# A decoder layer on one core: plain chunks moved inside a column pair, the tail of an up block spread, the residual kept in DRAM, a sixth raw tile

## The chip, the core and the metric

The kernel runs on one core of one Trainium2 chip. The core has a matrix engine (TensorE, PE in the profile; its weight loads are PEld), VectorE (DVE), ScalarE (ACT), GpSimd (POOL) and a queue processor (SyncE, SP), each with an instruction stream of its own. They wait for each other by semaphores. SP issues most of the DMA transfers, GpSimd the accumulating ones. The metric is the device time of one execution in microseconds; the figure compared is the median of the runs.

## The reference

One layer on 256 tokens of width 2048, in float32:

```
hn = rmsnorm(h);  q, k, v, g_ret, xr, yr, g_a, g_b = split(hn @ w_in)
ret_out = silu(g_ret) * head_groupnorm(chunkwise_retention(rotary(q), rotary(k), v))   # 8 heads
rnn_out = gelu(yr) * rg_lru(causal_dwconv(xr))
h = h + (sigmoid(g_a) * (ret_out @ w_proj_ret) + sigmoid(g_b) * (rnn_out @ w_proj_rnn)) @ w_mix_out
h = h + cross_attention(rmsnorm(h), rmsnorm(mem))          # 4 heads, 256 memory tokens
gate, val = split(causal_dwconv(rmsnorm(h) @ w_up, 3 taps))   # 2 x 5632 wide
h = h + (silu(gate) * val) @ w_down
return rmsnorm(h)
```

## The kernel before

**Products.** Every operand is split into two float32r parts, hi and lo, and a product is hi*hi + hi*lo + lo*hi. The weights come from DRAM as one long stream of pieces of 1 MB: four 128-row blocks by 512 columns (a chunk). A chunk is loaded into a `raw` tile (L263), cast to `hi` on ScalarE (L284), and VectorE writes `lo = raw - hi` (L285). `prefetch` does this two chunks ahead of their use. There are five raw tiles and three each of `hi` and `lo`.

**Column pairs.** Two 512-column blocks that share rows form a pair, listed in `PAIR_UNITS`. The first half of the contraction (rows 0 to 7) is done with seven block products on sums of operands (q1 to q7, a form of Strassen's scheme), the second half (rows 8 to 15) with four plain chunks (p). A q chunk takes 12 matmuls (one of them handles 512 columns), a p chunk 24. Three raw tiles, A, B and C, are held through a pair: q5 adds a piece to A by an accumulating DMA on GpSimd's queue (L265), then VectorE does A += B (L292); q6 uses A; q7 adds a piece to B by the same kind of DMA; VectorE does A += C (L290), and q4 uses A. The order in time is q1, p, q3, p, q5, q2, q6, p, q7, q4, p. Three PSUM accumulators serve a pair: xz, yu and rw; each holds [128, 2, 512]. There are three such tiles in all, and each chunk of a single column block (`gemm_n`) or of a transposed product (`gemm_t`) takes from the same three.

**Which p does what.** In the kernel before, p comes as (column 1, rows 8 to 11), (column 1, rows 12 to 15), (column 0, rows 8 to 11), (column 0, rows 12 to 15). Column 1 adds to rw, column 0 to yu. `pair_add` adds the accumulators to the residual rows `hrow` (L427), `pair_out` writes them to new tiles (L454 to L472).

**Order of work.** `later(n, fn)` puts a piece of side work n chunks ahead. The tile framework then orders each engine's instructions by priorities when the program is built; each engine runs its own list in that order. Tiles of the pool `bp` (25 of 4 KB per partition) hold operands, residual rows and the like; `tp` holds ten short-lived ones.

**Retention.** The eight heads come in two groups. In a group, q, k and v are computed, then a pair for the gates (`pair_out` at `O_G`). v of the first group is a `gemm_n`; `split_rows` reads its accumulator in two halves (L563 on ScalarE, L564 on VectorE). `retain` does the scores of a head (L518 on TensorE, L768, L769 on VectorE into `pret`), then the values; at the fourth head `normalise` takes the rsqrt (L608 on VectorE, the power L610 on GpSimd, L796) and scales the rows; `finish_head` transposes them (L530).

**Feed-forward.** `FF_PARTS` has groups of 4, 4 and 3 up blocks. An up block b is two `gemm_t` products, gate and value (`conv_up`): the accumulators are joined and scaled (L540, L541, L672), and a causal convolution of three taps follows (L1187, L1189). Then tanh (L1257), two products (L1258, L1259) and the split into a pair of `hid` tiles (L551, L552). In the first two groups `sums` makes the operands of the q chunks from the first four. A group of four is followed by two pairs of `ffn_w_down`, whose last quarter of the contraction is the two `hid` tiles of the fourth up block. The last group is followed by four plain `gemm_n`. All four `hrow` tiles stay in SBUF from cross-attention on.

Of the kernel before, what the change touches and what calls it, by code (L numbers as in the profile page):

```python
# [27 lines left out]
BW = 512  # L28
KC = 4
KH = 2  # L30
RAW_BUFS = 5
PART_BUFS = 3
AHEAD = 2
WARM = 8
# [60 lines left out]
def residual_plan(w):  # L95
# [5 lines left out]

PAIR_UNITS = [
    ("q1", "A", ("new", 0, 0)),
    ("p", None, (1, 8)),
    ("q3", "B", ("new", 1, 1)),
    ("p", None, (1, 12)),
    ("q5", "A", ("add", 0, 1)),
    ("q2", "C", ("new", 1, 0)),
    ("q6", "A", ("sum",)),
    ("p", None, (0, 8)),  # L110
    ("q7", "B", ("add", 0, 1)),
    ("q4", "A", ("sum",)),
    ("p", None, (0, 12)),
]

def entry_units(e):

    w, row, nk, cols = e[0], e[1], e[2], e[3:5]
    if len(cols) == 1:
        return [("p", None, "new", (w, tuple(row + (k + i) * P for i in range(KC)), cols[0])) for k in range(0, nk, KC)]  # L120
    out = []
    for kind, slot, a in PAIR_UNITS:
        if kind == "p":
# [29 lines left out]
def hybrid_layer(  # L153
# [17 lines left out]

    cp = ctx.enter_context(tc.tile_pool(name="cp", bufs=1))
    wp = ctx.enter_context(tc.tile_pool(name="wp", bufs=2))
    bp = ctx.enter_context(tc.tile_pool(name="bp", bufs=25))
    tp = ctx.enter_context(tc.tile_pool(name="tp", bufs=10))
    sp_ = ctx.enter_context(tc.tile_pool(name="sp", bufs=2))
    pm = ctx.enter_context(tc.tile_pool(name="pm", bufs=3, space=bass.MemoryType.PSUM))
# [205 lines left out]
    def pair_products(w, row, st, ss, c0, c1, out):  # L383

        xz, yu, rw = acc(), acc(), acc()
        x, z, y, u, r, w_ = (t[:, i, :] for t in (xz, yu, rw) for i in range(2))
        where = {
            "q1": (x, "a", 0, 0), "q2": (y, "a", 1, 0), "q3": (r, "s", 3, 0), "q4": (u, "a", 1, 1),
            "q5": (z, "s", 0, 0), "q6": (x, "s", 1, 0), "q7": (x, "s", 2, 0),
        }  # L390
        begun, plain = set(), 0

        def run(os_, opss, parts):
            for o, ops in zip(os_, opss):
                upper_n(o[0], ops, parts, o[1] not in begun)
                begun.add(o[1])
            for o, ops in zip(os_, opss):
                lower_n(o[0], ops, parts, True)

        names = {"q1": "x", "q2": "y", "q3": "r", "q4": "u", "q5": "z", "q6": "x", "q7": "x"}  # L400
        e = (w, row, NT, c0, c1)
        for kind, parts in units(*e):
            if kind == "p":
                k0 = 8 + 4 * (plain % 2)
                run(
                    (((r, "r"), (w_, "w")), ((y, "y"), (u, "u")))[plain // 2],
                    [
                        [halves(st[(k0 + k) // 2], k % 2, slice(tt * P, (tt + 1) * P)) for k in range(KC)]
                        for tt in range(2)
                    ],  # L410
                    parts,
                )
                plain += 1
            else:
                o, t, j, tt = where[kind]
                if t == "a":
                    ops = [halves(st[k], j, slice(tt * P, (tt + 1) * P)) for k in range(KC)]
                else:
                    ops = [(ss[k][:, 0, j * P : (j + 1) * P], ss[k][:, 1, j * P : (j + 1) * P]) for k in range(KC)]
                run(((o, names[kind]),), (ops,), parts)  # L420
            with tc.high_priority(URGENT):
                out(f"p{plain}" if kind == "p" else kind, x, z, yu, rw)

    def pair_add(w, row, st, ss, c0, c1, h0, h1):

        def add(o, i, op=ALU.add):
            dve.tensor_tensor(out=o, in0=o, in1=i, op=op)  # L427

        def out(kind, x, z, yu, rw):
            if kind == "q1":  # L430
                add(h0[:, 0, :], x)
            elif kind == "q5":
                later(3, lambda: add(h1, rw))
                later(4, lambda: add(h1, z[:, None, :].to_broadcast([P, 2, BW])))
            elif kind == "q6":
                add(h1[:, 0, :], x, ALU.subtract)
            elif kind == "q7":
                add(h0[:, 1, :], x)
                add(h1[:, 1, :], x, ALU.subtract)
            elif kind == "p4":  # L440
                add(h0, yu)

        pair_products(w, row, st, ss, c0, c1, out)

    def pair_out(w, st, ss, c0, r=None):
# [30 lines left out]
        def out(kind, x, z, yu, rw):  # L476
            if kind == "q1":
                copy(o0[:, 0, :], x, 0)
            elif kind == "q5":
                for tt in range(2):  # L480
                    copy(o1[:, tt, :], z, tt)
                later(3, lambda: add(o1, rw))
            elif kind == "q6":
                less(o1[:, 0, :], x, 0)
            elif kind == "q7":
                copy(o0[:, 1, :], x, 1)
                less(o1[:, 1, :], x, 1)
            elif kind == "p4":
                add(o0, yu)

        pair_products(w, 0, st, ss, c0, c0 + BW, out)
# [264 lines left out]
    def retain(g, qr, kr, vs, dec, gates):  # L756
# [4 lines left out]
        def scores(hh):  # L761
# [2 lines left out]
            product(sc[:, 0:S], halves(k, hh % 2, slice(0, P)), halves(q, hh % 2), True, True)  # L764
            late = slice(P, S)
            product(sc[:, S : S + P], halves(k, hh % 2, late), halves(q, hh % 2, late), True, True)
            pr_ = tp.tile([P, 384], F32, tag="pret", bufs=2, name=nm("pret"))
            dve.tensor_tensor(out=pr_[:, 0:S], in0=sc[:, 0:S], in1=dec[:, hh, :], op=ALU.mult)  # L768
            dve.tensor_tensor(out=pr_[:, S:384], in0=sc[:, S:384], in1=dec[:, hh, 0:P], op=ALU.mult)  # L769
            phi, plo = (tp.tile([P, 384], F32R, tag="tmp", name=nm("ps")) for _ in range(2))  # L770
# [4 lines left out]
        def values(hh, phi, plo):  # L775
# [12 lines left out]
                dve.bn_aggr(out=stats[:, 2 * hh + tt, :], in_=bn[:, tt, :])  # L788
            raws.append(rc)
            if hh == 3:  # L790
                later(2, normalise)

        def normalise():
            rstd = rsqrt_small(stats[:, :, 1], 8, 1.0, GN_EPS).rearrange("p (h t) -> p h t", t=2)
            for tt in range(2):
                dve.tensor_scalar_mul(rstd[:, :, tt], rstd[:, :, tt], rs0[:, tt : tt + 1])  # L796
# [381 lines left out]
    later(1, lambda: spread_tokens(rs2))  # L1178


    def conv_up(c0, b, dst):
        for pr, a in enumerate(gemm_t("ffn_w_up", 0, h2s, NT, c0 + b * BW)):
            z = scaled(a, "uz")
            for j in range(2):
                t = c0 // P + 4 * b + 2 * pr + j
                y = dst[:, 2 * pr + j, :]
                act.activation(y, z[:, j, :], AF.Identity, scale=pf[:, 2, t : t + 1], bias=pf[:, 3, t : t + 1])  # L1187
                for s in range(1, 3):
                    dve.scalar_tensor_tensor(  # L1189
                        out=y[:, s:S], in0=z[:, j, 0 : S - s], scalar=pf[:, 2 - s, t : t + 1], in1=y[:, s:S],  # L1190
                        op0=ALU.mult, op1=ALU.add,
                    )

    def down(b0, hid, b, final):

# [43 lines left out]
    def finish(b):  # L1239

        for tt in range(2):
            y = hrow[b][:, tt, :]
            square(y, ss3[:, tt, b : b + 1])
            dve.tensor_tensor(out=y, in0=y, in1=wfin[b // 2][:, b % 2, :], op=ALU.mult)

    b0 = 0
    for part, nb_ in enumerate(FF_PARTS):
        final = part == len(FF_PARTS) - 1
        hid, hid_sums = [], []
        for b in range(b0, b0 + nb_):  # L1250
            gt, vl = big([P, 4, S], s="fg"), big([P, 4, S], s="fv")
            conv_up(0, b, gt)
            conv_up(FF, b, vl)
            for pr in range(2):
                cs = slice(2 * pr, 2 * pr + 2)
                th, o = tmp("ft"), tmp("fo")
                act.activation(th, gt[:, cs, :], AF.Tanh, scale=0.5)  # L1257
                dve.scalar_tensor_tensor(out=o, in0=th, scalar=1.0, in1=gt[:, cs, :], op0=ALU.add, op1=ALU.mult)  # L1258
                dve.tensor_tensor(out=o, in0=o, in1=vl[:, cs, :], op=ALU.mult)  # L1259
                hid.append(split_pair(o, 0.5))  # L1260
                if nb_ == 4 and len(hid_sums) < KC:
                    hid_sums.append(sums(o, 0.5))
        if final:
            wfin = []
            for i in range(2):
# [48 lines left out]
```

## Time and profile before

| | |
|---|---|
| runs | 2009.12, 2009.64, 2011.54 us; median 2009.64 |
| profiled execution | 2011.54 us, span 2009.8 us |
| instructions | 24882 |
| DMA | 430.97 MB, mean 214 GB/s |
| granted TensorE clock | 0.998 on average |

The page has busy times by engine, the span in 40 slices, DMA queues, the chain that ended last, and groups of instructions. A row of the instructions in order of time reads: start, duration, engine, line, operation, output<-inputs, shape, count; in brackets the idle time of that engine before it and what ended it. Successive matmuls overlap in these rows: a matmul's own duration is about 0.39 us, while in a full stream starts follow each other at shorter distance, so lengths are taken from start to start.

### The profile page before, as it was taken

What the parts mean: (1) busy time and instruction counts of PE and PEld (TensorE: products, weight loads), DVE (VectorE), ACT (ScalarE), POOL (GpSimd) and SP (SyncE); (2) the same over time, 40 slices, a digit from 0 to 9 for tenths busy, and PEclk for the clock granted to TensorE, in tenths of its full rate; (3) what the DMA queues carried; (4) which work ended last, traced back from release to release, by engine and by line L of the source; (5) the groups of instructions that cost most, each with busy time, mean ns of one, the idle gap of its engine ahead of it and who ended that gap; (6) DMA issues with size and microseconds to landing.
All of it is one profiled execution on the core that took longest, in us unless ns stands there. A gap on an engine that the chain in (4) does not pass through costs nothing.

```text
span 2009.8 us, 24882 instructions
## 1 busy us (share of the span) xinstructions
PE 1989.9 (99%) x10072; PEld 1691.7 (84%) x10072; DVE 1585.2 (79%) x1588; ACT 1158.7 (58%) x1167; POOL 43.0 (2%) x52
## 2 busy tenths in 40 slices
PE   9999999999999999999999999999999999999998
PEld 7888888888888888888888888888878888788887
DVE  6798797889985886768888768777787787886765
ACT  6565656767665554566766556555544555544552
POOL 0000000000000000000000000000000000000000
PEclk9999999999999999999999999999999999999999
DMA  9664674655977775877886647655567555584552
GB/s 369 237 226 140 229 245 176 210 202 145 295 245 246 214 246 189 262 249 234 267 246 204 254 130 223 233 187 196 182 197 238 194 189 188 170 264 173 200 198 84
DMA packets 76003, 430.97 MB, mean 214 GB/s; under 512 B 8304, under 2 KB 13040, under 8 KB 28144
## 3 DMA queue, kind: packets, MB, share of 16 engines
q1 hardware_dynamic: 68608, 384.81, 52.2%
q0 software_dynamic: 5760, 41.95, 11.5%
q10 hardware_dynamic: 1520, 2.63, 0.4%
q8 instruction: 79, 1.29, 0.2%
q14 instruction: 36, 0.29, 0.0%
HBM read 418.87 MB, written 10.49 MB: 214 GB/s over the span
## 4 chain that ended last, share of the span: by engine, by line
PE 91%; DVE 5%; DMA 1%; issue 1%; ACT 1%; POOL 0%; SPq 0%; POOLq 0%; ACTq 0%; DVEq 0%
PE acc L349 37%; PE acc L360 17%; PE acc L361 17%; PE acc L367 16%; DVE lo L285 2%; PE sm L518 2%; DMA raw<-in_wall 1%; PE sm L530 1%; ACT hi L284 1%; PE acc L518 1%; PE sm L892 1%; DVE raw L292 0%; DVE fv L1189 0%; DVE tb L718 0%; DMA xt<-in_mem_t 0%
## 5 line engine op out<-in xcount | busy, mean ns | idle before, releaser
L285 DVE TENSOR_TENSOR lo<-raw,hi 128x2048 fp32r<-128x2048 f32 (+1 forms) x420 | 950.7, 2268 | 299.1 <-ACT hi L284 286.0
L284 ACT CAST hi<-raw 128x2048 fp32r<-128x2048 f32 (+1 forms) x418 | 792.8, 1902 | 624.1 <-PE acc L361 292.6
L360 PE MATMUL acc<-hi,s 128*128 128x512 f32 x1336 | 523.3, 392 | 4.3 <-ACT hi L284 3.9
L361 PE MATMUL acc<-hi,s 128*128 128x512 f32 x1336 | 520.7, 390 | 0.2 <-DVE s L575 0.2
L349 PE MATMUL acc<-s,hi 128*128 128x512 f32 x2176 | 518.0, 391 | 2.2 <-DVE hi L282 1.1
L349 PEld LDWEIGHTS acc<-s,hi 128*128 128x128 f32 x2176 | 401.9, 188 | 82.1 <-ACT hi L284 1.8
L367 PE MATMUL acc<-lo,s 128*128 128x512 f32 x1336 | 340.1, 392 | 0.1
L360 PEld LDWEIGHTS acc<-hi,s 128*128 128x128 f32 x1336 | 251.0, 188 | 58.0 <-ACT hi L284 5.2
L367 PEld LDWEIGHTS acc<-lo,s 128*128 128x128 f32 x1336 | 250.1, 188 | 53.6 <-DVE lo L285 0.5
L361 PEld LDWEIGHTS acc<-hi,s 128*128 128x128 f32 x1336 | 251.0, 188 | 52.2 <-DVE s L575 1.0
L349 PEld LDWEIGHTS acc<-s,lo 128*128 128x128 f32 x2176 | 277.0, 191 | 9.9 <-DVE lo L285 1.3
L349 PE MATMUL acc<-s,lo 128*128 128x256 f32 x2176 | 282.9, 283 | 0.5 <-DVE lo L285 0.5
L360 PE MATMUL acc<-hi,ss 128*128 128x512 f32 x320 | 127.2, 397 | 3.6 <-DVE o L470 1.7
L361 PE MATMUL acc<-hi,ss 128*128 128x512 f32 x320 | 125.5, 392 | 0.0
L367 PE MATMUL acc<-lo,ss 128*128 128x512 f32 x320 | 86.0, 390 | 0.0
L540 ACT COPY c<-acc 128x512 f32<-128x512 f32 x68 | 39.2, 578 | 75.2 <-PE acc L349 74.9
L360 PEld LDWEIGHTS acc<-hi,ss 128*128 128x128 f32 x320 | 60.6, 189 | 18.2 <-ACT hi L284 2.5
L361 PEld LDWEIGHTS acc<-hi,ss 128*128 128x128 f32 x320 | 60.6, 189 | 12.2
L367 PEld LDWEIGHTS acc<-lo,ss 128*128 128x128 f32 x320 | 60.0, 188 | 12.7
L265 POOL DMA_DIRECT2D raw<-in_wall x40 | 35.2, 879 | 1574.2 <-DVE lo L285 845.2
L427 DVE TENSOR_TENSOR nat<-nat,acc 128x512 f32<-128x512 f32 (+1 forms) x49 | 44.0, 910 | 6.7 <-PE acc L367 6.7
L290 DVE TENSOR_TENSOR raw<-raw,raw 128x2048 f32<-128x2048 f32 x20 | 45.8, 2288 | 0.4
(233 smaller groups left out, 1242.6 us busy)
## 6 DMA issues: line engine op xcount, KB each, us to landing
raw<-in_wall SPq DMA_DIRECT2D x333, 1024.0 KB, 4.9
raw<-in_wall POOLq DMA_DIRECT2D x40, 1024.0 KB, 8.0
xt<-in_x_t SPq DMA_DIRECT2D x11, 256.0 KB, 7.0
raw<-in_wall SPq DMA_DIRECT2D x5, 512.0 KB, 8.5
nat<-in_x ACTq DMA_DIRECT2D x4, 512.0 KB, 9.8
ret<-hd SPq DMA_DIRECT2D x8, 256.0 KB, 5.1
rnn<-rn SPq DMA_DIRECT2D x8, 256.0 KB, 3.1
kt<-ret SPq DMA_DIRECT2D x8, 256.0 KB, 5.6
```

The lines of the kernel that those rows point to most:

```text
L265: pool.dma_start(out=raw, in_=src, accum_op=ALU.add)
L284: act.copy(hi[:, a:b], raw[:, a:b])
L285: dve.tensor_tensor(out=lo[:, a:b], in0=raw[:, a:b], in1=hi[:, a:b].bitcast(F32), op=ALU.subtract)
L290: dve.tensor_tensor(out=to, in0=to, in1=by, op=ALU.add)
L349: pe.matmul(a, part, sx, start=k == 0 and t == 0, stop=k == nk - 1 and t == 0, skip_group_check=True)
L360: pe.matmul(o, h, hi, start=start and kk == 0, stop=False, skip_group_check=True)
L361: pe.matmul(o, l, hi, start=False, stop=False, skip_group_check=True)
L367: pe.matmul(o, h, lo, start=False, stop=stop and kk == KC - 1, skip_group_check=True)
L427: dve.tensor_tensor(out=o, in0=o, in1=i, op=op)
L518: pe.matmul(o, a, b, start=start and i == 0, stop=stop and i == 2, skip_group_check=True)
L530: pe.transpose(t[:, j, tt * P : (tt + 1) * P], rows[:, tt, k + j * P : k + (j + 1) * P], ident)
L540: act.copy(c, a[:, :, S:BW])
```

## The change

- **Plain chunks.** In `PAIR_UNITS` the four p units get names p0 to p3 and another order: (column 1, rows 8 to 11), (column 0, rows 8 to 11), (column 1, rows 12 to 15), (column 0, rows 12 to 15). The last quarter of the contraction is now used by the third and fourth p. q units and all positions stay.
- **Last up block.** `conv_up` is parted into `up` (product, join, scale) and `conv`; tanh, products and split go into `hidden`. In the fourth up block of a group of four, `conv` of the value half and `hidden` are put behind the second and the fourth chunk of the first `ffn_w_down` pair; else they run at once. In all up blocks both halves are joined and scaled before the first convolution.
- **Residual.** Before the first up block `hrow` is written to DRAM (`fkept`), and read back in the last up block of each group: all four in the last group, else two there and two in the first pair (after its fifth chunk). After each pair of `ffn_w_down` its two blocks are written again. All this goes by SP's queue.
- **Tiles.** `RAW_BUFS` 5 to 6, `bp` 25 to 24; `pret` takes its tile from the common tag `tmp` and no longer from two of its own.
- **Retention.** `normalise` is parted: the rsqrt runs one chunk earlier than before, the rest one chunk later.

```diff
-RAW_BUFS = 5
+RAW_BUFS = 6
...
 PAIR_UNITS = [
     ("q1", "A", ("new", 0, 0)),
-    ("p", None, (1, 8)),
+    ("p0", None, (1, 8)),
     ("q3", "B", ("new", 1, 1)),
-    ("p", None, (1, 12)),
+    ("p1", None, (0, 8)),
     ("q5", "A", ("add", 0, 1)),
     ("q2", "C", ("new", 1, 0)),
     ("q6", "A", ("sum",)),
-    ("p", None, (0, 8)),
+    ("p2", None, (1, 12)),
     ("q7", "B", ("add", 0, 1)),
     ("q4", "A", ("sum",)),
-    ("p", None, (0, 12)),
+    ("p3", None, (0, 12)),
 ]
...
-    bp = ctx.enter_context(tc.tile_pool(name="bp", bufs=25))
+    bp = ctx.enter_context(tc.tile_pool(name="bp", bufs=24))
...
+        rows = {"p0": (8, (r, "r"), (w_, "w")), "p1": (8, (y, "y"), (u, "u"))}
+        rows.update({"p2": (12,) + rows["p0"][1:], "p3": (12,) + rows["p1"][1:]})
...
-            elif kind == "p4":
+            elif kind == "p3":
...
-            pr_ = tp.tile([P, 384], F32, tag="pret", bufs=2, name=nm("pret"))
+            pr_ = tp.tile([P, 384], F32, tag="tmp", name=nm("pret"))
...
-                later(2, normalise)
-
-        def normalise():
+                later(1, rsqrt)
+
+        def rsqrt():
             rstd = rsqrt_small(stats[:, :, 1], 8, 1.0, GN_EPS).rearrange("p (h t) -> p h t", t=2)
+            later(1, lambda: normalise(rstd))
+
+        def normalise(rstd):
...
+    def up(c0, b):
+        return [scaled(a, "uz") for a in gemm_t("ffn_w_up", 0, h2s, NT, c0 + b * BW)]
+
+    def conv(c0, b, pr, z, dst):
+        for j in range(2):
...
+    def put_rows(n, bs):
+        for b in bs:
+            sp.dma_start(out=fkept[n, b], in_=hrow[b])
+
+    def get_rows(n, bs):
+        for b in bs:
+            hrow[b] = big([P, 2, BW], s="nat")
+            sp.dma_start(out=hrow[b], in_=fkept[n, b])
+
+    def hidden(gt, vl, pr, summed):
...
+    put_rows(0, range(4))
...
         for b in range(b0, b0 + nb_):
             gt, vl = big([P, 4, S], s="fg"), big([P, 4, S], s="fv")
-            conv_up(0, b, gt)
-            conv_up(FF, b, vl)
...
+            for pr, z in enumerate(up(0, b)):
+                conv(0, b, pr, z, gt)
+            if b + 1 == b0 + nb_:
+                later(0, lambda part=part, n=2 if paired else 4: get_rows(part % 2, range(n)))
+            for pr, z in enumerate(up(FF, b)):
+                def finish_up(b=b, pr=pr, z=z, gt=gt, vl=vl, paired=paired):
+                    conv(FF, b, pr, z, vl)
+                    hidden(gt, vl, pr, paired)
+
+                if paired and b + 1 == b0 + nb_:
+                    later(1 + 2 * pr, finish_up)
+                else:
+                    finish_up()
...
             for b in (0, 2):
+                if b == 0:
+                    later(4, lambda part=part: get_rows(part % 2, (2, 3)))
                 pair_add("ffn_w_down", b0 * BW, hid, hid_sums, b * BW, (b + 1) * BW, hrow[b], hrow[b + 1])
+                put_rows((part + 1) % 2, (b, b + 1))
```

More of the change, by code (lines that the diff above doesn't have):

```diff
@@ L122, in entry_units @@
     for kind, slot, a in PAIR_UNITS:
-        if kind == "p":
+        if kind[0] == "p":
             out.append((kind, slot, "new", (w, tuple(row + (a[1] + i) * P for i in range(KC)), cols[a[0]])))
@@ L390, in pair_products @@
         }
-        begun, plain = set(), 0
+        rows = {"p0": (8, (r, "r"), (w_, "w")), "p1": (8, (y, "y"), (u, "u"))}
+        rows.update({"p2": (12,) + rows["p0"][1:], "p3": (12,) + rows["p1"][1:]})
+        begun = set()
         def run(os_, opss, parts):
@@ L402, in pair_products @@
         for kind, parts in units(*e):
[L403 to L413, printed above, removed]
+            if kind in rows:
+                k0, *to = rows[kind]
+                ops = [
+                    [halves(st[(k0 + k) // 2], k % 2, slice(tt * P, (tt + 1) * P)) for k in range(KC)]
+                    for tt in range(2)
+                ]
+                run(to, ops, parts)
             else:
@@ L421, in pair_products @@
             with tc.high_priority(URGENT):
-                out(f"p{plain}" if kind == "p" else kind, x, z, yu, rw)
+                out(kind, x, z, yu, rw)
     def pair_add(w, row, st, ss, c0, c1, h0, h1):
@@ L487, in out @@
                 less(o1[:, 1, :], x, 1)
-            elif kind == "p4":
+            elif kind == "p3":
                 add(o0, yu)
@@ L1178, in hybrid_layer @@
     later(1, lambda: spread_tokens(rs2))
[L1181 to L1192, printed above, removed]
+    def up(c0, b):
+        return [scaled(a, "uz") for a in gemm_t("ffn_w_up", 0, h2s, NT, c0 + b * BW)]
+    def conv(c0, b, pr, z, dst):
+        for j in range(2):
+            t = c0 // P + 4 * b + 2 * pr + j
+            y = dst[:, 2 * pr + j, :]
+            act.activation(y, z[:, j, :], AF.Identity, scale=pf[:, 2, t : t + 1], bias=pf[:, 3, t : t + 1])
+            for s in range(1, 3):
+                dve.scalar_tensor_tensor(
+                    out=y[:, s:S], in0=z[:, j, 0 : S - s], scalar=pf[:, 2 - s, t : t + 1], in1=y[:, s:S],
+                    op0=ALU.mult, op1=ALU.add,
+                )
     def down(b0, hid, b, final):
@@ L1244, in finish @@
             dve.tensor_tensor(out=y, in0=y, in1=wfin[b // 2][:, b % 2, :], op=ALU.mult)
+    fkept = dp.tile([2, 4, P, 2, BW], F32, name="fkept")
+    def put_rows(n, bs):
[6 more added lines that the diff above has]
+    def hidden(gt, vl, pr, summed):
+        cs = slice(2 * pr, 2 * pr + 2)
+        th, o = tmp("ft"), tmp("fo")
+        act.activation(th, gt[:, cs, :], AF.Tanh, scale=0.5)
+        dve.scalar_tensor_tensor(out=o, in0=th, scalar=1.0, in1=gt[:, cs, :], op0=ALU.add, op1=ALU.mult)
+        dve.tensor_tensor(out=o, in0=o, in1=vl[:, cs, :], op=ALU.mult)
+        hid.append(split_pair(o, 0.5))
+        if summed and len(hid_sums) < KC:
+            hid_sums.append(sums(o, 0.5))
+    put_rows(0, range(4))
     b0 = 0
@@ L1248, in hybrid_layer @@
         final = part == len(FF_PARTS) - 1
+        paired = nb_ == 4
         hid, hid_sums = [], []
@@ L1251, in hybrid_layer @@
             gt, vl = big([P, 4, S], s="fg"), big([P, 4, S], s="fv")
-            conv_up(0, b, gt)
-            conv_up(FF, b, vl)
[L1254 to L1262, printed above, removed]
+            for pr, z in enumerate(up(0, b)):
[10 more added lines that the diff above has]
+                    finish_up()
         if final:
```

## The prediction

> **What bounds the kernel.** I read the page's first part, then the waits of TensorE, then the stretches of single column pairs, then the instructions in order of time where TensorE stood still.
>
> ```profile
> span 2009.8 us, 24882 instructions
> PE 1989.9 (99%) x10072; PEld 1691.7 (84%) x10072; DVE 1585.2 (79%) x1588; ACT 1158.7 (58%) x1167; POOL 43.0 (2%) x52
> ```
>
> TensorE is busy for 99% of the span, and the change leaves its matmuls as they are: what can be won is the time in which it stands or runs slow. The stretches show where. A row is one stretch; the columns are its length, then busy time and (count) of matmul, weight load, DVE, ACT and POOL, then the granted clock, DMA share and GB/s.
>
> ```profile
> 97.20:139.78 42.58, 41.96 (x181) 33.45 (x180) 41.00 (x34) 26.92 (x24) 0.87 (x1) 1.00 0.62 198
> 1451.76:1497.75 45.99, 43.21 (x183) 34.68 (x181) 40.80 (x35) 25.92 (x21) 1.76 (x2) 0.96 0.60 190
> 1497.75:1538.55 40.80, 40.80 (x182) 33.78 (x180) 35.76 (x21) 21.07 (x12) 0.86 (x1) 1.00 0.81 254
> 1716.49:1760.88 44.39, 41.67 (x183) 33.46 (x182) 39.22 (x34) 25.95 (x21) 1.51 (x2) 1.00 0.60 194
> 916.80:923.03 6.23, 6.00 (x25) 4.30 (x24) 6.23 (x7) 4.43 (x5) 0.91 (x1) 1.00 0.25 30
> 1485.13:1489.35 4.22, 4.22 (x11) 3.34 (x12) 4.22 (x4) 1.75 (x1) 0.00 (x0) 0.60 0.87 307
> ```
>
> One pair is seven q chunks of 12 matmuls and four p chunks of 24, 180 in all. The third row is a pair without a stop: 40.80 us, so 40.80/180 = 0.227 us a matmul, 2.72 us a q chunk, 5.44 us a p chunk. The first `ffn_w_down` pair after four up blocks takes 45.99 us (5.19 lost), that of the second group 44.39 (3.59 lost), the first gate pair of retention 42.58 (1.78 lost).
>
> Why the down pair stops: TensorE, then VectorE, then ScalarE around 1470 us.
>
> ```profile
> 1474.68 0.50 PE L360 MATMUL acc<-hi,ss 128*128 128x512 f32 x1 [0.81 <-ACT hi L284]
> 1485.13 0.50 PE L360 MATMUL acc<-hi,s 128*128 128x512 f32 x1 [1.96 <-ACT hi L284]
> ```
> ```profile
> 1452.95 2.29 DVE L285 TENSOR_TENSOR lo<-raw,hi 128x2048 fp32r<-128x2048 f32 x1 [1.72 <-ACT hi L284]
> ...
> 1458.54 1.66 DVE L1189 SCALAR_TENSOR_TENSOR fv<-uz,pf,fv 128x255 f32<-128x255 f32 x4
> 1460.12 0.69 DVE L1259 TENSOR_TENSOR fo<-fo,fv 128x512 f32<-128x512 f32 x1
> 1460.72 0.68 DVE L1258 SCALAR_TENSOR_TENSOR fo<-ft,fg 128x512 f32<-128x512 f32 x1
> ...
> 1463.12 2.28 DVE L285 TENSOR_TENSOR lo<-raw,hi 128x2048 fp32r<-128x2048 f32 x1
> 1465.33 0.69 DVE L552 SCALAR_TENSOR_TENSOR s<-fo,s 128x512 fp32r<-128x512 f32 x1
> ...
> 1470.33 2.29 DVE L292 TENSOR_TENSOR raw<-raw,raw 128x2048 f32<-128x2048 f32 x1
> ```
> ```profile
> 1460.99 0.63 ACT L551 ACTIVATE s<-fo 128x512 fp32r<-128x512 f32 x1
> ...
> 1472.73 3.71 ACT L284 CAST hi<-raw 128x2048 fp32r<-128x2048 f32 x2 [8.27 <-DVE raw L292]
> 1481.38 5.50 ACT L284 CAST hi<-raw 128x2048 fp32r<-128x2048 f32 x3 [4.93 <-PE acc L361]
> ```
>
> L292 (A += B) gates everything: q6 casts A (1472.73), and only then may the accumulating load add to B, which q7 casts at 1481.38. L292 ends at 1472.62, 20.9 us into the pair, because the whole tail of the last up block (L1189, L1258, L1259, L552) stands before it on VectorE. TensorE waits for q6 (0.81) and again behind p (1.96); then the last row of stretches: 11 matmuls in 4.22 us at clock 0.60.
>
> **The change, part by part.** Starts that follow each other give the pace: 0.60 us per 512-wide operation (1460.12 to 1460.72), 2.21 per L285 (1463.12 to 1465.33), 1.58 per four L1189, 1.84 per ScalarE cast.
>
> *Spread work and late plain chunks.* In the order of the changed program these stand on VectorE between the L285 of q3 and L292: L541, L427, L672, L285 of p1, four L1189, L1258, L285 of q5, L1259. From 1455.16: 0.6+0.6+0.6+2.21+1.58+0.6+2.21+0.6 = 9.0, so L292 runs 1464.2 to 1466.4, 6.2 us earlier. q6's cast can start then and TensorE, which reaches q6 five chunks and 21.8 us into the pair (1473.5), doesn't wait. The plain chunk on the last quarter is now p2, at 1476.3, and there the new stop is: the second `hid` tile that it multiplies is split on ScalarE behind the cast of q7, which waits for the accumulating load. From the end of L292 to q7's cast before: 1481.38 - 1472.62 = 8.76; so now 1466.4 + 8.8 = 1475.2, cast to 1477.0, L551 (0.6) to 1477.6, L552 to 1478.3. p2 needs the low half after five matmuls (1477.4), so 0.8 us stop. L290 and q4's cast follow (1478.3 + 2.2 + 1.9 = 1482.4), and p2 ends at 1482.5: no second stop, and no clock loss from it. The pair: 40.80 + 0.8 = 41.6. Won: 5.19 - 0.8 = 4.4. The second group has the same shape:
>
> ```profile
> 1739.43 0.50 PE L360 MATMUL acc<-hi,ss 128*128 128x512 f32 x1 [0.80 <-ACT hi L284]
> ...
> 1749.84 0.50 PE L360 MATMUL acc<-hi,s 128*128 128x512 f32 x1 [1.93 <-ACT hi L284]
> ```
>
> It won't lose more than 0.8 either: 3.59 - 0.8 = 2.8. Bounds for the remaining stop: 0 (the load lands a little earlier) to 2.8 each (both stops shown above); I take 0.8 from the sum.
>
> [...]
>
> ```profile
> raw<-in_wall POOLq DMA_DIRECT2D x40, 1024.0 KB, 8.0
> ```
>
> [...]
>
> *The same order in other pairs.* In `xa_w_q` the late quarter is late too: 24 matmuls take 6.23 us in the stretch at 916.80, against 24 x 0.227 = 5.44. With p1 on the third quarter the 0.8 is won.
>
> But all pairs pay for it in PSUM: yu is now written by p1, the fourth chunk, not by q2, the sixth. Where yu's bank belonged to a `gemm_n` that is read out late, p1 waits. By bank addresses and readout times this is so in one place, the first gate pair of retention (bank of v, read by L564):
>
> ```profile
> 107.14 1.07 PE L367 MATMUL acc<-lo,ss 128*128 128x512 f32 x4
> ...
> 116.50 0.50 PE L360 MATMUL acc<-hi,s 128*128 128x512 f32 x1
> ...
> 145.32 0.81 PE L518 MATMUL sm<-s,s 128*128 128x256 f32 x6
> ```
> ```profile
> 108.83 0.68 DVE L549 TENSOR_TENSOR s<-ta,s 128x512 fp32r<-128x512 f32 x1
> ...
> 115.70 0.74 DVE L564 SCALAR_TENSOR_TENSOR v<-acc,ro,v 128x512 fp32r<-128x512 f32 x1
> ```
>
> Before, q2 started at 116.50, right behind L564 (116.44), after p and q5 had filled the time. In the changed order TensorE has, after q3 (107.14 + 4 x 0.227 = 108.05): twelve score matmuls, q5, then p1. The scores need L549 (109.51), so 1.5 us stop; they take 1.3 (six took 0.65 to the next start); q5 takes 2.7; that fills to 113.5, or to 114.6 if q5 waits for the readout of q1's x; p1 at 116.5. In all 116.5 - 108.05 - 1.3 - 2.7 = 4.4 us stand. The 1.78 that this pair loses now (at and behind 116.50) lies behind the new stop and goes. Cost: 4.4 - 1.8 = 2.6. Bounds: 0 (v read out in time) to 4.4 plus a slow clock of 1.7, which is what the stretch at 1485.13 lost (4.22 - 11 x 0.227).
>
> *rsqrt one step earlier, normalise one later.*
>
> ```profile
> 198.05 0.36 DVE L796 TENSOR_SCALAR ro<-ro,ro 128x4 f32<-128x4 f32 x2 [1.57 <-POOL ro L610]
> ...
> 201.31 0.68 DVE L470 TENSOR_TENSOR o<-o,acc 128x512 f32<-128x512 f32 x1
> ```
> ```profile
> 199.97 1.03 PE L530 MATMUL sm<-cid,rc 128*128 128x128 f32 x8
> 202.05 0.50 PE L360 MATMUL acc<-hi,ss 128*128 128x512 f32 x1 [1.05 <-DVE o L470]
> ```
>
> VectorE waits 1.57 us for GpSimd's power; the q7 of that pair waits for the L470 behind it. In the new order the L285 and L470 stand ahead of L796, and L608 three large operations ahead: about 1.1 us won (bounds 0 and 1.2).
>
> *Residual in DRAM.* 24 transfers of 512 KB on SP's queue, 12 written and 12 read, 12.6 MB.
>
> ```profile
> SPq L263 <- DVE lo L285: 1414.0, 284, 19.6
> nat<-hkept SPq DMA_DIRECT2D x4, 512.0 KB, 6.9
> ```
> ```profile
> 1490.02 3.72 ACT L284 CAST hi<-raw 128x2048 fp32r<-128x2048 f32 x2 [3.14 <-PE acc L361]
> ```
>
> SP stands 1414 us waiting for raw tiles, so room is there. The one risky issue is the read of the last two blocks: it waits for the up block's gt and vl (the second L1259, about 1473.7), and raw loads for the next pair queue behind it. With 6.9 us and one more load behind they land by about 1486; their casts begin at 1490.02 and 1491.9, TensorE wants the second at 1500.5. Cost 0; the cover is 12 us to TensorE. VectorE's first add into h0 also waits for its read, which stands in SP's queue ahead of the pair's fifth load, before the pair starts: 0. Writes wait for adds already done when their turn comes: 0. The sixth raw tile lets loads go out one chunk earlier; no stop above waits for a plain load, so 0. The smaller pool and the shared tmp tag: 0, shown only as the moved scores above. The rw sum is now read just when p2 ends; VectorE has 40.80 - 35.76 = 5 us free in an undisturbed pair: 0, at most 2 in a pair.
>
> **Sum.** 4.4 + 2.8 + 0.8 + 1.1 - 2.6 = 6.5 us. The profiled execution took 2011.54 us (span 2009.8), so 2005.0; the median of the three runs is 1.9 us lower, 2009.64, and from it **2003.1 us**.
>
> **Rivals.**
> (a) The retention stop costs nothing, since the queue ahead of L564 also gets shorter: 2003.1 - 2.6 = 2000.5. Against it: the order up to L564 is unchanged. 0.12.
> (b) The clock falls at the retention stop: +1.7, 2004.8. The stretch at 1485.13 shows it behind stops of 0.81 and 1.96; behind the like stops at 1739.43 and 1749.84 the clock in its stretch stays 1.00. 0.18.
> [...]
> (c) The down pair's stop only moves to p2: if L292 comes 3 us later than I add up, or the load is that much longer, each pair loses 3.8: 2003.1 + 6 = 2009.1, no change. For it: ScalarE's order with `hid` behind q7. 0.15.
> (d) Slower: the read of the last two residual blocks holds the raw loads. It decides from 12 us on; each us beyond costs TensorE one, in both groups; 6 us beyond gives 2003.1 + 12 = 2015. Against it: gt and vl are free before p2 starts. 0.08.
> The forecast keeps 0.47.
>
> **Chances and range.** A difference under 0.2% (4.0 us) is about what can't be told from no change. Faster: 0.47 + 0.12 + 0.18, less 0.15 for terms missed, 0.62; same: (c) and 0.09 of what is missed, 0.24; slower: (d) and the rest, 0.14. Range 2000.0 to 2009.2: down to (a) with half a us, up to (c). The likeliest case alone: 2001.5 to 2005.
>
> **What would show it.** Right: down pairs of about 41.6 us with L292 some 14.7 us in and one stop at the second plain chunk's `hid`; stops before the first scores and before p1 near 108 to 116.5; no wait for L470 near 202; SP's reads of the residual never ahead of a TensorE wait. Wrong: a new wait of TensorE for raw loads, a low clock near 110, or a down pair still above 44 us.

## The result

The median of the runs goes from 2011.38 us to 2006.07 us. The ratio is 0.9973, with a 95% interval of 0.9965 to 0.9982: faster by 0.27%. The medians differ by 5.3 us; the interval goes from 3.6 to 7.0 us. The forecast was 6.5 us. It was made from a median of 2009.64, and more runs of the same kernel put that at 2011.38, so the forecast time of 2003.1 lies 3 us too low for two reasons: 1.7 us of base and 1.2 us of gain. The interval is too wide to tell 5.3 from 6.5; the stretches of the profiled executions, below, show more.

The profiled execution of the changed kernel took 2005.55 us. First part of its page:

```profile
span 2003.8 us, 24972 instructions
PE 1988.4 (99%) x10072; PEld 1692.9 (84%) x10072; DVE 1583.4 (79%) x1588; ACT 1157.9 (58%) x1167; POOL 47.0 (2%) x52
```

TensorE has the same 10072 matmuls. The difference is time in which it stood or ran slow.

**The stretches.** A row gives the stretch, its length, then busy time by engine, the granted clock, DMA share and GB/s. Two stretches are cut wider than in the prediction, because score matmuls move between a pair and the products behind it. The first runs from the gate pair's first matmul through all scores of the first heads, the next goes on past the q7 that waited for L470. Before:

```profile
97.16:170.84 73.68, 72.87 (x371) 61.16 (x369) 63.55 (x67) 43.55 (x41) 1.73 (x2) 1.00 0.64 206
170.84:244.36 73.52, 72.39 (x359) 60.85 (x360) 60.54 (x61) 44.50 (x48) 3.65 (x3) 1.00 0.61 200
```

After: the same two, the 24 matmuls in `xa_w_q`, the two down pairs of the first group, and the first down pair of the second.

```profile
96.66:173.00 76.34, 72.46 (x370) 61.54 (x369) 63.45 (x67) 43.87 (x41) 1.73 (x2) 1.00 0.60 198
173.00:245.21 72.21, 72.14 (x359) 60.82 (x360) 60.53 (x61) 44.52 (x48) 7.65 (x3) 1.00 0.62 204
917.48:922.92 5.44, 5.44 (x26) 4.51 (x24) 5.44 (x6) 3.81 (x6) 0.10 (x1) 1.00 0.02 9
1451.60:1493.70 42.10, 41.67 (x182) 33.64 (x181) 39.81 (x35) 26.56 (x21) 1.76 (x2) 1.00 0.69 227
1493.70:1535.03 41.33, 41.07 (x181) 33.72 (x180) 35.25 (x21) 20.75 (x12) 0.86 (x1) 1.00 0.85 261
1712.98:1754.88 41.90, 41.65 (x183) 33.63 (x181) 39.78 (x35) 26.57 (x21) 1.76 (x2) 1.00 0.67 230
```

| place | before | after | won | forecast |
|---|---|---|---|---|
| first down pair, group 1 | 45.99 | 42.10 | 3.9 | 4.4 |
| first down pair, group 2 | 44.39 | 41.90 | 2.5 | 2.8 |
| 24 matmuls in `xa_w_q` | 6.23 | 5.44 | 0.8 | 0.8 |
| stretch with normalise | 73.52 | 72.21 | 1.3 | 1.1 |
| first gate pair and its scores | 73.68 | 76.34 | -2.7 | -2.6 |
| second down pair, group 1 | 40.80 | 41.33 | -0.5 | 0 |
| sum | | | 5.3 | 6.5 |

The spans differ by 6.0 us. Of what is missing in the table, 0.5 us lies ahead of the gate pair, which starts at 96.66 instead of 97.16; the last part of this text shows how much that start wanders by itself. So that the sum of the table meets the 5.3 us of the medians to a tenth is in part luck: the table is of one execution of each kernel, and the row of the second down pair, as shown further below, is an event of one execution.

**The down pair.** VectorE, ScalarE and TensorE in order of time in the changed kernel (start, duration, engine, line, operation, output<-inputs):

```profile
1463.98 2.28 DVE L293 TENSOR_TENSOR raw<-raw,raw 128x2048 f32<-128x2048 f32 x1
...
1473.37 0.68 DVE L1265 TENSOR_TENSOR fo<-fo,fv 128x512 f32<-128x512 f32 x1
...
1477.36 0.69 DVE L551 SCALAR_TENSOR_TENSOR s<-fo,s 128x512 fp32r<-128x512 f32 x1 [1.10 <-ACT s L550]
```
```profile
1474.88 1.91 ACT L285 CAST hi<-raw 128x2048 fp32r<-128x2048 f32 x1 [2.96 <-DMA raw<-in_wall]
1476.70 0.62 ACT L550 ACTIVATE s<-fo 128x512 fp32r<-128x512 f32 x1
```
```profile
1477.38 0.50 PE L361 MATMUL acc<-hi,s 128*128 128x512 f32 x1 [0.20 <-ACT s L550]
1478.10 0.50 PE L362 MATMUL acc<-hi,s 128*128 128x512 f32 x1 [0.22 <-DVE s L551]
```

A += B (now L293) ends 14.7 us into the pair instead of 20.9, and q6's cast no longer holds TensorE. What is left is the split of the last `hid` tile: its input is ready at 1474.05, but L550 stands behind the cast of q7 in ScalarE's list and ends at 1477.32. TensorE stops for it twice, at two matmuls that follow each other: for the high half and then for the low.

**The gate pair of retention.** TensorE, then VectorE:

```profile
109.06 1.12 PE L517 MATMUL sm<-s,s 128*128 128x256 f32 x8 [0.89 <-DVE s L548]
111.37 0.50 PE L361 MATMUL acc<-hi,ss 128*128 128x512 f32 x1 [1.20 <-ACT o L453]
...
115.99 0.50 PE L361 MATMUL acc<-hi,s 128*128 128x512 f32 x1 [1.60 <-DVE v L563]
```
```profile
112.99 2.28 DVE L293 TENSOR_TENSOR raw<-raw,raw 128x2048 f32<-128x2048 f32 x1
115.19 0.74 DVE L563 SCALAR_TENSOR_TENSOR v<-acc,ro,v 128x512 fp32r<-128x512 f32 x1
```

Three stops follow each other: before the later scores, before q5, and before p1, which starts right when the second L563 has read v out of the bank (115.93).

### The profile page after: what moved, and what is told of

The parts are those of the page before. It is cut to its first block, busy times and chain, and to the rows that moved or that the text cites. A ratio compares the mean times of both kernels' runs of the same rounds, so it can differ in the third digit from the quotient of the medians.

```text
span 2003.8 us, 24972 instructions
## 1 busy us (share of the span) xinstructions
PE 1988.4 (99%) x10072; PEld 1692.9 (84%) x10072; DVE 1583.4 (79%) x1588; ACT 1157.9 (58%) x1167; POOL 47.0 (2%) x52
## 4 chain that ended last, share of the span: by engine, by line
PE 91%; DVE 3%; issue 2%; DMA 2%; ACT 1%; POOLq 0%; SPq 0%; ACTq 0%; POOL 0%; DVEq 0%
PE acc L350 38%; PE acc L361 16%; PE acc L368 16%; PE acc L362 16%; DMA raw<-in_wall 2%; PE sm L517 2%; DVE lo L286 1%; PE sm L529 1%; PE acc L517 1%; ACT hi L285 1%; PE sm L894 1%; DVE raw L293 0%; DVE tb L717 0%; DVE ta L721 0%; DVE fv L1192 0%
## 5 line engine op out<-in xcount | busy, mean ns | idle before, releaser
L286 DVE TENSOR_TENSOR lo<-raw,hi 128x2048 fp32r<-128x2048 f32 (+1 forms) x420 | 951.0, 2267 | 295.0 <-ACT hi L285 288.1
```

Of the source, the lines that this page charges most:

```text
L286: dve.tensor_tensor(out=lo[:, a:b], in0=raw[:, a:b], in1=hi[:, a:b].bitcast(F32), op=ALU.subtract)
```

## The experiments

All compare with runs of the kernel before on the same chip; ratios carry their 95% interval. Times are best read as ratios, since the kernel before had medians of 2011.2 to 2012.2 us in the three sets of these runs. The changed kernel's ratio is 0.9973.

### The order alone

The kernel before, with only the plain chunks exchanged.

```diff
-    ("p", None, (1, 12)),
+    ("p", None, (0, 8)),
...
-    ("p", None, (0, 8)),
+    ("p", None, (1, 12)),
```

> The kernel before with nothing changed but the order of the plain chunks (last quarter of the contraction in the third and fourth p). Theory: the order wins nothing in the down pairs by itself, since L292 still stands behind the whole tail of the up block: both stops at q6 and q7 stay (4.9 and 3.3 us above pace), xa_w_q gains its 0.7, the first gate pair of retention loses 2.45 more than before (4.2 instead of 1.7). In all about 2011.4 + 1.7 = 2013.1 us, ratio to before 1.0009. Rival: the order alone takes the stops out of the down pairs; then 2011.4 + 1.7 - 6 = about 2007.

Measured: ratio 1.0008 (1.0000 to 1.0017), 2013.18 us. The stretches of its gate pair with the scores, and of the first down pair of each group; then its scores:

```profile
96.73:173.08 76.35, 72.52 (x371) 61.54 (x369) 63.46 (x67) 43.88 (x41) 1.73 (x2) 1.00 0.60 199
1453.16:1497.52 44.36, 41.43 (x182) 33.55 (x181) 39.19 (x34) 25.91 (x21) 1.50 (x2) 1.00 0.59 194
1716.27:1762.49 46.22, 43.13 (x182) 34.72 (x181) 40.84 (x35) 25.90 (x21) 1.76 (x2) 0.96 0.59 189
```
```profile
109.13 1.12 PE L518 MATMUL sm<-s,s 128*128 128x256 f32 x8 [0.89 <-DVE s L549]
```

The order pays the full 2.7 us in retention and wins nothing in the down pairs: 44.36 and 46.22 are within 0.3 us of the two lengths of before, with the groups exchanged. The rival that the order takes the stops away falls. The scores, too, stand inside the gate pair here, though `pret` still has its own tiles: it is the order that moves them, not the shared tag, as the prediction had it.

### The spread taken away

```diff
-                if paired and b + 1 == b0 + nb_:
-                    later(1 + 2 * pr, finish_up)
-                else:
-                    finish_up()
+                finish_up()
```

> The changed kernel, but the convolution, products and split of the last up block run at once, as before; order, residual in DRAM and sixth raw tile stay. Theory: the two down pairs lose what they have won (3.9 and 2.5 us), about 2006.1 + 6.4 = 2012.5 us; if the slow clock that followed the stop in the kernel before doesn't come, about 2010.8. The stop of TensorE stands at the cast of q6 and of q7 again. Rival: the sixth raw tile or the late plain chunks did it, and the spread is worth nothing: 2006.

Measured: ratio 1.0001 (0.9992 to 1.0010), 2011.87 us. The down pairs:

```profile
1451.72:1497.67 45.95, 43.07 (x182) 34.71 (x181) 40.82 (x35) 25.90 (x21) 1.76 (x2) 0.96 0.67 213
1716.41:1760.94 44.53, 41.47 (x183) 33.57 (x181) 39.20 (x34) 25.95 (x21) 1.51 (x2) 1.00 0.66 216
```

And the stops in the first of them:

```profile
1474.64 0.50 PE L361 MATMUL acc<-hi,ss 128*128 128x512 f32 x1 [0.97 <-ACT hi L285]
1485.03 0.50 PE L361 MATMUL acc<-hi,s 128*128 128x512 f32 x1 [1.91 <-ACT hi L285]
```

Both pairs are as long as before, with the same two stops. The whole gain of the down pairs hangs on the spread; the sixth raw tile and the order keep none of it.

### The spread under the old order

The old order in all pairs; the two pieces of work behind the second and third chunk, since the fourth chunk needs them.

```diff
-    ("p1", None, (0, 8)),
+    ("p1", None, (1, 12)),
...
-    ("p2", None, (1, 12)),
+    ("p2", None, (0, 8)),
...
-                    later(1 + 2 * pr, finish_up)
+                    later(1 + pr, finish_up)
```

> The changed kernel with the old order of the plain chunks in all pairs; the last up block's work is spread as far as that order allows (second and third chunk of the pair instead of second and fourth, since the fourth chunk already multiplies it). Theory: in the program the scheduler puts q5 and q2 ahead of parts of this plain chunk; adding up VectorE's list, TensorE then stops about 0.7 us at q6's cast, 1.9 at q2's low half and 1.0 at q6's low half, 3.6 in a down pair instead of 1.0; the gate pair of retention has its old 1.7 again. In all 2006.1 + 2 x 2.6 - 2.45 = 2008.8 us. Rival one: the spread does all by itself and the order only costs: 2003.6. Rival two: the plain chunk waits in order for its operands, some 9 us in each pair: 2019.

Measured: ratio 0.9985 (0.9976 to 0.9994), 2008.41 us. The down pairs, and the two larger of the stops in the first:

```profile
1452.68:1496.39 43.71, 41.91 (x183) 33.49 (x181) 41.42 (x35) 26.66 (x21) 1.76 (x2) 1.00 0.69 227
1715.13:1758.82 43.69, 41.90 (x182) 33.48 (x181) 41.42 (x35) 26.66 (x21) 1.76 (x2) 1.00 0.69 226
```
```profile
1472.38 1.19 PE L368 MATMUL acc<-lo,s 128*128 128x512 f32 x4 [0.85 <-DVE lo L286]
1474.45 0.50 PE L361 MATMUL acc<-hi,s 128*128 128x512 f32 x1 [0.88 <-ACT hi L285]
```

Without the order the spread still wins 2.3 and 0.7 us in the down pairs; with it 3.9 and 2.5. The stops are 2.9 us a pair where 3.6 were added up. So, beside the spread and with the later place that it allows for the second piece of work, the order is worth 1.6 + 1.8 us here and 0.8 in `xa_w_q`, and costs 2.7 in retention: 1.5 us in all by place, and the ratios (0.9985 and 0.9973) say 2.4. It pays, but only together with the spread. With the second piece at the same, earlier place under both orders (the experiment "The last `hid` tile one chunk earlier", below: 40.88 and 40.90 us) the order is worth 2.8 us in each down pair.

### The cause of the stop in retention, two ways

First, the old order in the one pair of `w_in` that starts at `O_G`, the gate pair of the first group.

```diff
     for kind, slot, a in PAIR_UNITS:
+        if cols[0] in OLD_ORDER and w == "w_in":
+            a = {"p1": (1, 12), "p2": (0, 8)}.get(kind, a)
...
+        if c0 in OLD_ORDER and w == "w_in":
+            rows["p1"], rows["p2"] = rows["p2"], rows["p1"]
```

> The changed kernel with the old order of the plain chunks in one pair alone, the first gate pair of retention. Theory: the stop at the bank of v is caused by the order; the scores go back behind the pair, the pair loses 1.7 instead of 4.2 us: 2006.1 - 2.45 = 2003.6 us, ratio to before 0.9961. Rival: the readout of v is late for another reason, and TensorE stops elsewhere in the pair: 2006.

Measured: ratio 0.9961 (0.9948 to 0.9973), 2003.73 us. The stretch is back at what it was:

```profile
97.15:170.91 73.76, 72.87 (x371) 61.16 (x369) 63.55 (x67) 43.64 (x41) 1.73 (x2) 1.00 0.62 205
```

Second, the order kept, but v read out ahead of the rotation of k.

```diff
-                turned.append(rotated(a))
                 vs.append(split_rows(v, rs0))
+                turned.append(rotated(a))
```

> The changed kernel, order of the plain chunks as changed, but in the first group of retention split_rows of v is called ahead of rotated (the accumulator of v is read before the rotation of k instead of behind it). In VectorE's list the two L563 of this v then stand eight and six places further ahead, some 5 us; nothing else of the pair's order on VectorE is taken away. Theory: the stop before the fourth chunk is the bank of v and nothing else, so it goes without the old order of chunks: 2006.1 - 2.4 to 4.0 = about 2003 us, and no TensorE wait on L563. Rival: another late reader (the copy of q1's x, the rotated k) takes its place: 2006.

Measured: ratio 0.9971 (0.9960 to 0.9982), 2005.16 us. No wait for L563 is left, and the stretch is 1.35 us shorter, not 2.4 or more. VectorE and TensorE of this kernel:

```profile
96.28:171.27 74.99, 72.64 (x370) 61.32 (x369) 63.46 (x67) 43.49 (x41) 1.73 (x2) 1.00 0.62 203
```
```profile
106.39 0.75 DVE L563 SCALAR_TENSOR_TENSOR v<-acc,ro,v 128x512 fp32r<-128x512 f32 x1
...
111.07 4.49 DVE L286 TENSOR_TENSOR lo<-raw,hi 128x2048 fp32r<-128x2048 f32 x2
115.47 2.29 DVE L293 TENSOR_TENSOR raw<-raw,raw 128x2048 f32<-128x2048 f32 x1
```
```profile
119.80 0.51 PE L361 MATMUL acc<-hi,ss 128*128 128x512 f32 x1 [0.79 <-ACT hi L285]
130.13 0.50 PE L361 MATMUL acc<-hi,s 128*128 128x512 f32 x1 [1.42 <-ACT hi L285]
```

The bank of v was the cause of p1's wait: L563 now ends at 107.14 and p1 no longer waits. But the edit is not as narrow as it looks: the scores move on TensorE too, to 118.21 us and later. And A += B now stands behind one more L286 and ends 21.5 us into the pair (117.76 - 96.28) instead of 18.6 (115.27 - 96.66), and the casts of q6 and q7 hold TensorE. Half the theory holds. As the rival has it, another stop takes its place, but it is these casts and not one of the late readers that the rival named. (1.35 us is less than the interval can tell; the stretches show it.)

### The last `hid` tile one chunk earlier

```diff
-                    later(1 + 2 * pr, finish_up)
+                    later(1 + pr, finish_up)
```

> The changed kernel with the second half of the last up block's work put behind the third chunk of the down pair instead of the fourth. TensorE's list stays as it is; on ScalarE the split of the last hid tile (L550) then stands ahead of the cast of q7, on VectorE four L1192 and L1264 stand ahead of the lo of q2. Theory: the stop in p2 (0.98 in the first group, 0.80 in the second) is this one place in ScalarE's list; it goes: 2006.1 - 1.8 = 2004.3 us. Rival one: VectorE is the limit, the lo of q2 or q6 comes late instead, a stop of 1 to 2 us in each pair: 2006 to 2008. Rival two: q7's cast, now behind, is late: about 2006.

Measured: ratio 0.9964 (0.9951 to 0.9976), 2003.73 us. ScalarE, and the down pair of the first group:

```profile
1472.73 0.63 ACT L550 ACTIVATE s<-fo 128x512 fp32r<-128x512 f32 x1
1476.20 1.92 ACT L285 CAST hi<-raw 128x2048 fp32r<-128x2048 f32 x1 [2.84 <-PE acc L362]
```
```profile
1452.44:1493.32 40.88, 40.88 (x183) 33.72 (x181) 39.69 (x35) 26.64 (x21) 1.76 (x2) 1.00 0.70 233
```

With L550 ahead of q7's cast the pair runs at TensorE's pace, 40.9 us, and the second group's does too. The stop that the prediction left in each pair is this one place in a list, and VectorE is not the limit.

### The residual in SBUF

No transfers of `fkept`; five raw tiles and 26 tiles of `bp`.

```diff
-            sp.dma_start(out=fkept[n, b], in_=hrow[b])
+            pass
...
-            hrow[b] = big([P, 2, BW], s="nat")
-            sp.dma_start(out=hrow[b], in_=fkept[n, b])
+            pass
```

> The changed kernel with the residual kept in SBUF: no transfer of fkept, five raw tiles instead of six and 26 tiles of bp instead of 24, which is the same space. Theory: the transfers cost only the 0.5 us before q7 of the second pair of the first group, whose accumulating loads landed in 10.5 and 8.8 us beside them instead of 8.7 and 8.0: 2005.6 us. Rival: moving 12.6 MB more costs 1 us or more somewhere, or the sixth raw tile is worth as much: 2005 or less, or 2007 and more.

Measured: ratio 0.9977 (0.9967 to 0.9987), 2006.57 us: no gain, no loss that can be told. The first down pair is 42.15 us long, as after.

### Five raw tiles beside the transfers

```diff
-RAW_BUFS = 6
+RAW_BUFS = 5
```

> The changed kernel with five raw tiles instead of six, the residual in DRAM as changed. TensorE's and VectorE's lists stay as they are. Theory (prediction): the sixth tile is worth nothing, no stop of TensorE waits for a plain load: 2006. Rival: it covers the reads of the residual, which stand in the same queue ahead of raw loads; without it the chunk behind them comes late in both groups, 1 to 4 us each: 2008 to 2014.

Measured: ratio 0.9975 (0.9965 to 0.9985), 2006.17 us. Beside the transfers the sixth tile is worth nothing that can be told. Six tiles without the transfers were not run.

### normalise in one part

```diff
-                later(1, rsqrt)
+                later(2, rsqrt)
...
-            later(1, lambda: normalise(rstd))
+            normalise(rstd)
```

> The changed kernel with normalise in one part again, rsqrt a chunk later and the scaling a chunk earlier, as in the kernel before. Theory: TensorE waits for L469 near 202 us again, 1.2 us in the profile of the kernel before and none after: 2006.1 + 1.2 = 2007.3 us. Rival: the readout before q7 is late because of the order of chunks or the shared tmp tag, and the split of normalise is worth nothing: 2006.

Measured: ratio 0.9978 (0.9969 to 0.9987), 2008.05 us; beside 0.9973 about 1 us, within the scatter. The trace is clearer: the stretch has its old length, and the wait for L469 is there.

```profile
174.30:247.87 73.57, 72.65 (x360) 60.87 (x360) 60.63 (x61) 44.52 (x48) 3.64 (x3) 1.00 0.62 200
205.52 0.50 PE L361 MATMUL acc<-hi,ss 128*128 128x512 f32 x1 [0.84 <-DVE o L469]
```

### The two edits together

The old order in the first gate pair, and the last `hid` tile one chunk earlier.

> The changed kernel with two edits that were tried alone: the old order of the plain chunks in the first gate pair of retention, and the second half of the last up block's work behind the third chunk of the down pair. Theory: the two places are far apart and their gains add up, 2.4 and 1.8 us: 2006.1 - 4.2 = 2001.9 us, ratio to before 0.9953, no TensorE stop left in the down pairs and 1.8 us in the gate pair. Rival: the starting stretch or the clock gives part of it back: 2003.7, as each alone.

Measured: ratio 0.9956 (0.9942 to 0.9969), 2002.57 us. Gate pair and first down pair:

```profile
96.62:139.23 42.61, 41.97 (x181) 33.48 (x180) 41.00 (x34) 27.00 (x24) 0.87 (x1) 1.00 0.61 198
1449.74:1490.61 40.87, 40.87 (x183) 33.72 (x181) 39.68 (x35) 26.66 (x21) 1.77 (x2) 1.00 0.69 233
```

By place the gains add up: the two stretches are as short as with each edit alone. This version beats both kernels: 8.8 us (0.44%) against the kernel before, some 3.4 us against the changed one. Expected were 4.2 beyond the changed one; the intervals can't tell these two apart.

The same two edits, and the residual in SBUF with five raw tiles:

> The same two edits, and the residual kept in SBUF with five raw tiles and 26 tiles of bp. Theory: neither the transfers nor the sixth raw tile is worth anything, so the time is that of the two edits, 2001.9 us. Rival: with the stops gone the transfers or the sixth tile begin to matter: 2001 or less, or 2003.5 and more.

Measured: ratio 0.9956 (0.9943 to 0.9968), 2002.42 us. The transfers and the sixth tile together are not needed for the gain, here either.

## Why the prediction was right, point by point

- **The bound.** Right. TensorE's work stayed, and the table accounts for the gain by its stops alone.
- **Down pairs, 4.4 and 2.8.** Right in place, mechanism and order, 0.5 and 0.3 too high. L293 ran at 1463.98 to 1466.26, forecast 1464.2 to 1466.4. The one stop is in p2, at the second `hid` tile, as worked out: L550 forecast to end at 1477.6, measured 1477.32. But L550 and L551 each stop TensorE, at successive matmuls, and behind them it starts again slower than its pace (0.34 us to the next start, then 0.24, against 0.227), so 1.3 and 1.1 us are lost instead of 0.8. The sum counted the wait for the low half alone. The experiment with L550 moved shows that nothing else is in this term; the one without the spread shows that the other parts bring none of the gain by themselves. One count in the working is off without harm: q6 is reached six chunks into the pair, not five; its 21.8 us are those of six.
- **`xa_w_q`, 0.8.** Right: 5.44 us.
- **The gate pair, -2.6.** Right: -2.7, at the bank of v. The pair with its scores is 46.66 us long: 40.80 of products, 1.3 of scores and 4.6 of stops, where 4.4 were added up. Both edits that remove the reason remove the wait for L563. One remark fell: the scores move with the order, not with the tag.
- **rsqrt, 1.1.** Right: 1.3, and the stretch has its old length again when the edit is undone.
- **Residual, sixth raw tile, pools: 0.** Right: leaving out the transfers or the sixth tile moves the ratio by 0.0004 or less, inside the intervals.
- **What the sum left out.** 0.5 us in the second down pair of the first group of the profiled execution. In the trace of after TensorE waits there for a readout behind L286, whose piece came late (ScalarE's cast of it, at 1519.07, had waited 5.07 us for the load):

```profile
1524.05 0.47 PE L361 MATMUL acc<-hi,ss 128*128 128x512 f32 x1 [0.26 <-DVE nat L426]
```

The transfers alone don't explain it. With the residual in SBUF (and five raw tiles) the pair is 40.80 us long, without a stop; but the execution with the longest such stop is of the version with the two edits that has no transfers, here its pair:

```profile
1490.47:1532.93 42.46, 41.07 (x182) 33.71 (x181) 35.30 (x21) 20.66 (x12) 0.87 (x1) 1.00 0.77 232
```

Nor does it belong to the change as such. Four versions keep the transfers and have the changed kernel's order and spread in both down pairs: the old order in the gate pair, v read out first, five raw tiles, and normalise in one part. Their first pairs are 42.1 to 42.4 us long, and in all four the second is 40.80. With the old order in the gate pair:

```profile
1492.15:1532.95 40.80, 40.80 (x181) 33.79 (x180) 36.47 (x21) 20.96 (x12) 0.86 (x1) 1.00 0.88 275
```

What goes with the stop is the median landing time of the two accumulating loads of that pair. In the view of DMA issues over this stretch, before, after, and the version with the longest stop:

```profile
raw<-in_wall POOLq DMA_DIRECT2D x2, 1024.0 KB, 8.3
```
```profile
raw<-in_wall POOLq DMA_DIRECT2D x2, 1024.0 KB, 9.6
```
```profile
raw<-in_wall POOLq DMA_DIRECT2D x2, 1024.0 KB, 10.2
```

At 8.3 there is no stop, nor at 8.4 to 8.8 in the five versions just named, nor at 9.4 in the two edits with the transfers; at 9.6 the pair is 0.5 us longer and at 10.2 it is 1.7. By these the pair's slack is used up near 9.5. Why the loads landed later in these two executions stays open.
- **The rivals.** (a), no stop in retention, fell: the order alone shows all 2.7 us of it. (c), the stop only moves to p2, fell: the stop is at p2, but with 1.3 and 1.1 us instead of (c)'s 3.8, since L293 and the load came when they were forecast (q7's cast at 1474.88, forecast 1475.2). (d), residual reads hold the raw loads, fell with the two experiments on transfers and raw tiles. (b), a slow clock at the retention stop, needs the last part: the clock stayed at 1.00 there in the profiled execution of the changed kernel; it fell there in the profiled executions of three of its versions (0.96 over the 46.66 us of the pair without the spread), and cost nothing there.

## What to carry over

When an engine's list holds a long block of side work just ahead of one operation on which the next products wait, moving that work by a few chunks can win all of the stop if the consumer of the side work is moved later as well (with the consumer where it was, the down pairs won 2.3 and 0.7 us of 5.2 and 3.6). Look at what the moved consumer pulls forward, here an accumulator written two chunks earlier, whose bank was still to be read out. Check the pairs that share the order one by one: the same exchange won 0.8 us in one pair and lost 2.7 in another, and an exception for that pair won the 2.7 back. A remaining stop of about one microsecond can be one instruction's place in one list, and is worth looking for there before anything larger is tried.

## What was not expected of the hardware

**The clock fell behind three of six like stops.** The down pair with its two stops (about 1 and 2 us) is six times in the traces: two groups, in the kernel before, with the order alone, and without the spread. In three of the six the granted clock falls behind the second stop, to a mean of 0.79 over 8 us (1482 to 1490 or 1747 to 1755); in the other three it stays at 1.00 there. It fell in one group of each execution: the first, the second, the first. The order alone, from the first matmul behind the second stop of each group:

```profile
1486.50:1490.70 4.20, 4.20 (x18) 3.44 (x19) 4.20 (x4) 2.67 (x2) 0.00 (x0) 1.00 0.82 291
1749.80:1754.00 4.20, 4.17 (x13) 3.24 (x14) 4.20 (x4) 1.79 (x1) 0.00 (x0) 0.67 0.76 289
```

The length of the stop doesn't tell the two cases apart here: the clock fell behind one of 1.91 us (without the spread, first group) and not behind one of 1.93 us (the kernel before, second group). What decides is not shown. In the kernel before seven slow matmuls follow each other from 1486.04 us; they start 0.43 us apart, against 0.227, and the granted clock from 1486.04 to 1489.03 is 0.50. The 0.60 in the prediction's stretch from 1485.13 is a mean with matmuls at full pace in it.

**A slow clock in front of a later wait cost nothing here.** In the retention stop the clock fell too, for instance without the spread:

```profile
96.50:143.16 46.66, 44.40 (x193) 36.28 (x192) 43.08 (x40) 28.20 (x26) 0.87 (x1) 0.96 0.60 203
110.00:114.20 4.20, 3.00 (x8) 2.40 (x8) 4.20 (x4) 1.85 (x4) 0.00 (x0) 0.60 0.54 224
```

The pair is 46.66 us long there with a mean clock of 0.96, and from 96.66 to 143.32, 46.66 us as well, in the changed kernel, where the clock stayed at 1.00. The clock fell in this pair in two more traces: to 0.59 in a stretch of 4.20 us with the residual in SBUF, and to 0.96 over the pair with the last `hid` tile one chunk earlier. With the latter the pair is 46.66 us long, and with the former the stretch that goes on through all scores is 76.34 us long, both as in the changed kernel. The slow matmuls lie ahead of the wait for L563, and that wait is shorter where they are slow: 1.6 us in the changed kernel, 0.2 without the spread. So rival (b) named an event that did occur, and its price of 1.7 us was wrong.

**The start wanders by more than some edits are worth.** The gate pair's first matmul came at 96.66 us in the changed kernel and at 97.95 with normalise in one part, whose instructions are the same up to there; the latter had this wait in its first chunks, which the former had not.

```profile
11.29 0.73 PE L350 MATMUL acc<-s,hi 128*128 128x512 f32 x2 [0.88 <-ACT hi L285]
```

A single span therefore doesn't decide on an edit of 1 or 2 us; the stretch in which it lies does.
